# The first stage of a two-layer step: modulation loads in 1 KB runs, and five tiles of 128 tokens for the narrow projection

## The chip, the cores and the metric

The kernel runs on one core of a Trainium2 chip. The metric is the device time of one execution in microseconds (us). In the tables of the profile PE is the matrix engine (TensorE), DVE the vector engine, ACT the scalar engine, POOL the GpSimd engine and SP the engine that issues most of the DMAs.

## The reference

Two layers, the first a stick-breaking attention, the second a gated linear attention, work on 512 prompt tokens and 8 x 16 sample tokens, 640 tokens in all, with a model width of 2048, in float32. Each layer begins like this:

```
shift, scale, gate = jnp.split(c @ w_ada[i] + b_ada[i], 3, axis=-1)
h = rmsnorm(x, norm_g[i]) * (1 + scale[:, None]) + shift[:, None]
...
q, k, v, zg = jnp.split(h @ w_in, 4, axis=-1)
...
x = x + gate[:, None] * y
```

`c` has 9 rows (one for the prompt, 8 for the samples), and `w_ada[i]` is 2048 x 6144. Layer 0 has `w_in` of 2048 x 8192. Layer 1 has it 2048 x 6160, with its own `q`, `k`, `v`, `r` and a 16-wide decay input. The outputs are the normed activations, the new keys and values, and the states.

## The kernel before

Activations stand with the model width on the partitions: `xT` and `h` are 16 k-tiles of 128 rows by 640 tokens. Every float32 product is made of three matmuls on a split operand: `halves` makes `hi` by a cast on ACT and `lo = x - hi` on DVE, and a product is hi*hi, hi*lo and lo*hi, accumulated in PSUM.

**The first stage** loads x, transposes it, and makes the row scales (to about 30 us). It then makes shift and scale of layer 0 in pieces (`ada0`, `ada_mod`). A piece takes the columns of n k-tiles (n/2 lower ones, j, and the same upper ones, j + 8), for shift and scale each, over all 2048 rows of `w_ada`. A load into a ring tile `ar` is 128 partitions by 4 blocks of 64n columns, so that an uninterrupted run is 256n bytes: 512 bytes for n = 2, 1 KB for n = 4. Narrow matmuls (L178, 32 columns stationary, each quarter of PE's columns its own block) add them up in a PSUM bank; a DVE copy (`ada_r`, L181) and transposes by PE (L185) follow, then DVE, POOL and ACT make `mod`, the shifted and scaled k-tiles j and j + 8 (`scaled`, L247 to L253), and `part_up` splits them: the lower k-tile in two halves of 320 tokens, the upper whole. `part_up` also stores a half in DRAM (`h21_d`), on SP's queue. `add_up` makes sums and differences of quarters and their splits, which only later products read (`by_sevens`, which makes a product of 2 x 2 blocks from seven smaller ones).

Beside this runs `six` (L454): the first 512 columns of v, for which the 640 tokens stand as stationary tiles and the weights stream with 512 columns. For each j it needs the splits of k-tiles j and j + 8, and makes 6 token tiles x 2 k-tiles x 3 = 36 matmuls. The token tiles are 128, 128, 64, 128, 128 and 64 wide, since the lower k-tiles are held in halves of 320; the six accumulators hold five banks `mm` and the bank `z`. After the last j, L753 evacuates and SP stores (`v01`); then `by_sevens` (L520) takes the next projections.

The order on PE is the program's own: `drive` yields after each token tile, and `side.tick` puts in the next step of `ada0` when the planner's clock `pe["now"]` has passed its due time. `pace` sets such a time from the loads asked for so far, `side.every` the least distance of such steps, and `by` charges each matmul to that clock. `until` fills with side work until the planned `ready` time of j. SP, ACT, DVE and POOL take their instructions in an order that a scheduler makes.

**Layer 1** calls `six` again with all the k-tiles near at hand, the order of ACT, DVE and POOL being that of the code; its accumulators are evacuated as `vhi` and `vlo` (L1233), whose tiles have one buffer each, and stored before the next are made.

Of the kernel before, what the change touches and what calls it, by code (L numbers as in the profile page):

```python
# [15 lines left out]
P = 128  # L16
D = 2048
KT = D // P
NP = 512
# [22 lines left out]
def hybrid_step_kernel(ctx: ExitStack, tc: tile.TileContext, A: dict, O: list):  # L42
# [4 lines left out]
    dve = nc.vector  # L47


    pe = {"now": 0.0}  # L50

    mm, turn_block = nc.tensor.matmul, nc.tensor.transpose

    def by(l, r):

        n = r.free_size()
        if l.dtype == F32R:
            pe["now"] += n / 2400 + 0.0133
        elif l.free_size() <= 32:
            pe["now"] += n / 2400 + 0.01  # L60
        else:
            pe["now"] += n / 600 + 0.005
        return r
# [310 lines left out]
    class Quarters:  # L374
# [1 line left out]


        def __init__(self):
            self.lower, self.upper, self.whole = [None] * 8, [None] * 8, [None] * 8
            self.sums, self.exact = [[None] * 8 for _ in range(4)], [None] * 8  # L380

        def rows(self, kt, t0, w):
# [7 lines left out]

        def scale(self, i, j, xT, bc, pool=None):

            ts = self.exact[j] = [xT[kt] if pool is None else pool.tile([P, T], F32, tag="mod", name="mod", bufs=3)
                                  for kt in (j, 8 + j)]
            for t, kt in zip(ts, (j, 8 + j)):
                scaled(t, i, kt, xT[kt], bc)

        def part_up(self, i, j):

            (a0, a1), b = [self.exact[j][0][:, c] for c in hs], self.exact[j][1]  # L400
            store(h21_d[i][:, j, :], a1)
            self.lower[j], self.upper[j] = slot(j, (P, 2, HALF)), slot(8 + j, (P, 2, HALF))
            self.whole[j] = slot(16 + 2 * j), slot(17 + 2 * j)
            halves(self.lower[j][:, 0], self.lower[j][:, 1], a0)
            halves(self.upper[j][:, 0], self.upper[j][:, 1], a1)
            halves(*self.whole[j], b)

        def add_up(self, j, pool, places, gp=()):

# [19 lines left out]
                    self.upper[n + e] = slot(8 + n + e, (P, 2, HALF))  # L429
                    halves(self.upper[n + e][:, 0], self.upper[n + e][:, 1], r[:, e])  # L430

    tiles6 = [(0, P), (P, P), (256, 64), (320, P), (448, P), (576, 64)]

    def six(h, w, n0, acc, until, asked):


        src = w.rearrange("(kt p) n -> p kt n", p=P)

        def piece(j):
            asked()  # L440
            return wpiece(src[:, j:j + 9:8, n0:n0 + 512], 2, 512)

        nxt = piece(0)
        yield
        for j in range(8):
            until(j)
            wh, wl = nxt
            if j < 7:
                nxt = piece(j + 1)
            for i, (t0, n) in enumerate(tiles6):  # L450
                for e in range(2):
                    hi, lo = h.rows(j + 8 * e, t0, n)
                    for l, r, first, last in ((hi, wh, True, False), (hi, wl, False, False), (lo, wh, False, True)):
                        mm(acc[i][:n, :], l, by(l, r[:, e, :]), start=j == 0 and e == 0 and first,  # L454
                           stop=j == 7 and e == 1 and last)
                yield

# [216 lines left out]
    with tc.tile_pool(name="st", bufs=1, reuse_waits="tile") as st:  # L674
        for n, t in (("sh", sh_t), ("sc", sc_t)):
            t[0] = st.tile([P, KT, NSEQ], F32, name=f"{n}0")

        raw = {}
        crow = st.tile([120, P], F32, name="crow")
        c9 = st.tile([P, NSEQ, KT], F32, name="c9")  # L680
        for a in range(TOK):
            for hf in range(2):
                raw[a, hf] = sp.tile([P, 1024], F32, tag=f"s{2 * a + hf}", name="xr")
                load(raw[a, hf], x_src(a)[:, 1024 * hf:1024 * hf + 1024])
            if a == 0:
                load(crow[0:32, :], A["norm_g"].rearrange("l (k d) -> (l k) d", d=P))
                load(crow[32:48, :], A["gla_norm_g"].rearrange("l (k d) -> (l k) d", d=P))
                load(crow[48:56, :], A["gla_b_a"].rearrange("l (k d) -> (l k) d", d=P))
                load(crow[56:120, :], A["b_ada"][:, :2 * D].rearrange("l (k d) -> l k d", d=P))
                load(c9[:, 0, :], A["c_prompt"][0].rearrange("(p kt) -> p kt", kt=KT))  # L690
                load(c9[:, 1:, :], A["c_sample"].rearrange("r (p kt) -> p r kt", kt=KT))
        dve.tensor_copy(cT[:, :, :NSEQ], c9.rearrange("p r kt -> p kt r"))

        xT = [slot(kt if kt < 8 else 2 * kt, dt=F32, name="xT") for kt in range(KT)]
        bc = st.tile([P, T], F32, name="rstd_bc")
        for a in range(TOK):
            ss4 = st.tile([P, 4], F32, tag="ss4", name="ss4", bufs=2)
# [12 lines left out]
            rstd_row(st, ss, bc, a)  # L710
            if a == 2:
                tp = bank("tp")
                nc.tensor.transpose(tp[:, :120], crow, ident[:120, :120])
                dve.tensor_copy(cols, tp[:, :120])


        pe["now"] = 30.0
        come = {"n": 0}
        ready = {}

        def pace(n):
            come["n"] += n
            return max(0.0, 24.0 + 1.9 * come["n"] - pe["now"])

        def ring(tags):
            n = 0
            while True:
                tag = tags[n % len(tags)]
                yield ad_ring() if tag is None else sp.tile([P, 1024], F32, tag=tag, name="ar")
                n += 1  # L730

        early = ring(["s10", "s11", "s12", "s13", "s14", "s15", None, None])
        late = ring(["s12", "s13", "s14", "s15", None, None])
        last = ring(["s14", "s15", None, None])

        def ada0():
            for k0, n, r in ((0, 2, early), (1, 2, early), (2, 4, early), (4, 4, early), (6, 2, late), (7, 2, last)):
                yield from ada_mod(ad, lambda: next(r), 0, k0, n, "tp", 2, pace)
                for j in range(k0, k0 + n // 2):
                    h1.scale(0, j, xT, bc, st)  # L740
                    h1.part_up(0, j)
                    h1.add_up(j, st, (f"s{2 * j}", f"s{2 * j + 1}"))
                    ready[j] = pe["now"] + 6.5

        side.every = 1.0
        side.add(ada0())
        acc = [bank("mm") for _ in range(5)] + [bank("z")]
        drive(six(h1, w_in0, 2 * D, acc, lambda j: side.until(lambda: ready.get(j, 1e9) <= pe["now"]),
                  lambda: pace(1)))
        side.finish()  # L750
        for i, (t0, n) in enumerate(tiles6):
            t = slot(8 + i, (P, 512), F32, "v01")
            (dve.tensor_copy if i % 2 else nc.scalar.copy)(t[:n, :], acc[i][:n, :])  # L753
            for p in range(2):
                store(v_d[p][t0:t0 + n, :], t[:n, 256 * p:256 * p + 256])
            np_ = max(0, min(t0 + n, NP) - t0)
            if np_:
                store(vp_rows[t0:t0 + np_, 0:512], t[:np_, :])
            if np_ < n:
                store(vs_rows[max(t0, NP) - NP:t0 + n - NP, 0:512], t[np_:n, :])  # L760


    def rest_of_ada():
# [351 lines left out]
    with tc.tile_pool(name="o0", bufs=1, reuse_waits="tile") as po, ExitStack() as only_d:  # L1115
# [55 lines left out]
            if j == 6:  # L1171
                halves(wa[:, :, :16], wa[:, :, 16:], r)

        acc = [bank("mm") for _ in range(5)] + [bank("z")]
        gemm = six(h2, w_in1, 2 * NK, acc, until, lambda: None)
        next(gemm)
        side.finish()
# [14 lines left out]
        def make(j):  # L1192
            if j < 7:
                h2.scale(1, j + 1, xT, bc)
            if j < 8:
                h2.part_up(1, j)


        wa = pm.tile([P, 512], F32R, name="wa").rearrange("p (k n) -> p k n", k=KT)
# [23 lines left out]
        add_up()  # L1223
        queries = plain(h2, src, [(P * hh, leave_q(hh)) for hh in range(2)])

        for i, (t0, n) in enumerate(tiles6):
            if i == 2:
                next(queries)
            parts = [pm.tile([P, 512], F32R, tag=t, name=t) for t in ("vhi", "vlo")]
            halves(parts[0][:n, :], parts[1][:n, :], acc[i][:n, :])  # L1230
            for d in range(2):
                store(gv_d[0][d][t0:t0 + n, :], parts[d][:n, :].bitcast(F32))
        alr = pm.tile([96, 2, HALF], F32R, name="alr")  # L1233
        for nt in range(2):
            x = low[nt][:32, :HALF]
# [540 lines left out]
```

## Time and profile before

| | |
|---|---|
| time, median of 3 runs | 2637.93 us (2637.6 to 2638.26) |
| the profiled execution, its own time | 2633.23 us |
| its span (1.83 us lie around it) | 2631.4 us |
| PE busy | 2475.0 us, 94% of the span |
| DVE, ACT, POOL busy | 61%, 39%, 10% |
| DMA moved | 503.83 MB, mean 191 GB/s |

The span is divided by the profile in 40 slices of 66 us. PE is busy for nine tenths or more in nearly all of them; the slices in which it isn't are the first (6 tenths) and a few about the two attention stages. The views read here are the busy time in stretches, the instructions in order of time for one engine, the waits, and the chain of work that ended last.

### The profile page before, as it was taken

To read this page: it belongs to the slowest core of one execution; us is meant where nothing else is said; L and a number is where in the kernel's file an instruction comes from. 1 tells how busy PE (TensorE), PEld (TensorE's weight loads), DVE (VectorE), ACT (ScalarE), POOL (GpSimd) and SP (SyncE) were. 2 spreads that over 40 slices of the span, in tenths; PEclk is the share of its full clock that TensorE was granted. 3 is DMA by queue.
4 is the path that set the end of the run, shared out by engine and by line. 5 is a ranking of instruction groups with operands and counts; after the bars stand their busy time and mean duration, and the time that the engine had idled before them with its cause. 6 is when DMAs were issued, how large, how long until landed. Compare 5 with 4: busy or idle time off the path is not lost.

```text
span 2631.4 us, 43839 instructions
## 1 busy us (share of the span) xinstructions
PE 2475.0 (94%) x17393; PEld 2162.9 (82%) x17393; DVE 1597.8 (61%) x2429; ACT 1017.4 (39%) x1804; POOL 261.3 (10%) x537
## 2 busy tenths in 40 slices
PE   6999999999999989999999989999999998787998
PEld 4569999989999989787777767999999987675776
DVE  4555556555556646766776666666677564555556
ACT  4332222222223335555453453333333362464333
POOL 1200000000000000000000050000000134424300
PEclk8899999999999999999999989999999998999999
DMA  9966666766674366666665633344543577846554
GB/s 314 314 208 222 216 216 202 232 209 216 198 237 144 118 215 212 227 209 221 209 225 173 189 110 108 90 119 117 144 119 105 170 226 233 280 158 209 203 196 148
DMA packets 495358, 503.83 MB, mean 191 GB/s; under 512 B 26090, under 2 KB 416626, under 8 KB 495026
## 3 DMA queue, kind: packets, MB, share of 16 engines
q1 hardware_dynamic: 477426, 446.49, 53.7%
q0 software_dynamic: 17728, 54.54, 6.3%
q8 instruction: 137, 2.24, 0.3%
q14 instruction: 67, 0.55, 0.1%
HBM read 411.16 MB, written 89.78 MB: 190 GB/s over the span
## 4 chain that ended last, share of the span: by engine, by line
PE 74%; DMA 7%; DVE 7%; issue 5%; ACT 3%; POOL 3%; SPq 1%; ACTq 0%; POOLq 0%; DVEq 0%
PE ps_mm L520 41%; PE ps_mm L619 8%; PE ps_mm L454 4%; PE ps_mm L356 3%; PE ps_mm L575 3%; PE ps_tp L976 2%; PE ps_tp L944 1%; PE ps_z L920 1%; PE ps_z L178 1%; DMA ar<-in_w_ada_dram 1%; PE ps_z L218 1%; DVE wl L136 1%; PE ps_tp L1021 1%; PE ps_mm L1747 1%; PE ps_z L989 1%
## 5 line engine op out<-in xcount | busy, mean ns | idle before, releaser
L520 PE MATMUL ps_mm<-sums,wh 128*128 128x320 f32 x2880 | 642.2, 311 | 0.4 <-ACT wh L135 0.4
L520 PE MATMUL ps_mm<-h,wh 128*128 128x320 f32 x2160 | 484.7, 313 | 5.5 <-ACT wh L135 3.8
L520 PEld LDWEIGHTS ps_mm<-sums,wh 128*128 128x128 f32 x2880 | 479.4, 188 | 12.2 <-issue 9.0
L520 PE MATMUL ps_mm<-sums,wl 128*128 128x320 f32 x1440 | 445.3, 309 | 0.7 <-DVE wl L136 0.7
L520 PEld LDWEIGHTS ps_mm<-h,wh 128*128 128x128 f32 x2160 | 360.4, 188 | 22.0 <-issue 13.3
L136 DVE TENSOR_TENSOR wl<-wr,wh 128x1024 fp32r<-128x1024 f32 x191 | 233.9, 1226 | 234.0 <-ACT wh L135 233.0
L135 ACT CAST wh<-wb 128x1024 fp32r<-128x1024 f32 x180 | 188.9, 1049 | 460.2 <-PE ps_mm L520 389.6
L520 PE MATMUL ps_mm<-h,wl 128*128 128x320 f32 x1080 | 334.8, 310 | 2.2 <-DVE wl L136 2.2
L135 ACT CAST wh<-wr 128x1024 fp32r<-128x1024 f32 x191 | 200.1, 1049 | 330.4 <-PE ps_mm L520 201.1
L520 PEld LDWEIGHTS ps_mm<-sums,wl 128*128 128x128 f32 x1440 | 270.4, 188 | 1.0 <-DVE wl L136 1.0
L136 DVE TENSOR_TENSOR wl<-wb,wh 128x1024 fp32r<-128x1024 f32 x180 | 219.9, 1222 | 66.0 <-ACT wh L135 63.4
L619 PE MATMUL ps_mm<-wh,ogh 128*128 128x512 f32 x450 | 199.7, 444 | 15.5 <-ACT ogh L135 11.0
L575 PE MATMUL ps_mm<-h,wh 128*128 128x320 f32 x896 | 209.1, 321 | 3.5 <-DVE out L526 2.1
L520 PEld LDWEIGHTS ps_mm<-h,wl 128*128 128x128 f32 x1080 | 203.5, 188 | 2.9 <-DVE wl L136 2.9
L619 PE MATMUL ps_mm<-wh,ogl 128*128 128x512 f32 x450 | 180.4, 401 | 0.6 <-DVE ogl L136 0.4
L619 PE MATMUL ps_mm<-wl,ogh 128*128 128x512 f32 x450 | 180.4, 401 | 0.0
L575 PEld LDWEIGHTS ps_mm<-h,wh 128*128 128x128 f32 x896 | 153.0, 193 | 16.0 <-issue 11.3
L575 PE MATMUL ps_mm<-h,wl 128*128 128x320 f32 x448 | 140.9, 315 | 2.3 <-DVE wl L136 2.3
L454 PE MATMUL ps_mm<-wh,h 128*128 128x512 f32 (+1 forms) x320 | 113.4, 425 | 10.0 <-ACT h L135 7.1
L619 PEld LDWEIGHTS ps_mm<-wh,ogh 128*128 128x128 f32 x450 | 87.8, 195 | 41.7 <-ACT ogh L135 12.2
L858 DVE TENSOR_TENSOR_SCAN k<-k,zero_c 128x544 f32<-128x544 f32 (+4 forms) x96 | 93.3, 975 | 29.7 <-ACT k L854 17.5
L619 PEld LDWEIGHTS ps_mm<-wh,ogl 128*128 128x128 f32 x450 | 86.6, 192 | 21.7 <-DVE ogl L136 1.8
(306 smaller groups left out, 3912.4 us busy)
## 6 DMA issues: line engine op xcount, KB each, us to landing
ar<-in_w_ada_dram SPq DMA_DIRECT2D x160, 512.0 KB
wb<-in_sb_w_in_dram SPq DMA_DIRECT2D x84, 512.0 KB
kc<-in_cache_sb_k_dram SPq DMA_DIRECT2D x64, 512.0 KB
vc<-in_cache_sb_v_dram SPq DMA_DIRECT2D x64, 512.0 KB
wb<-in_gla_w_in_dram SPq DMA_DIRECT2D x51, 512.0 KB
wr<-in_gla_w_in_dram SPq DMA_DIRECT2D x45, 512.0 KB
wr<-in_sb_w_in_dram SPq DMA_DIRECT2D x44, 512.0 KB
ar<-in_w_ada_dram SPq DMA_DIRECT2D x64, 256.0 KB
```

Source lines behind the costliest of these rows:

```text
L135: nc.scalar.copy(hi, x)
L136: dve.tensor_tensor(lo, x, hi.bitcast(F32), op=ALU.subtract)
L178: mm(acc[32 * q:32 * q + 32, :w], cT[:, kt + m, :], by(cT[:, kt + m, :], rs[m // each][:, m % each, q, :]), start=kt + m == 0, stop=kt + m ...
L218: mm(acc[32 * j:32 * j + 32, :256], cT[:, kt + m, :], by(cT[:, kt + m, :], r[:, 256 * j:256 * j + 256]), start=kt + m == 0, stop=kt + m == ...
L356: mm(acc[a], l[:, c], by(l[:, c], r[:, k2, :]), start=kt == k0 and first, stop=kt == k0 + nk - 1 and last)
L454: mm(acc[i][:n, :], l, by(l, r[:, e, :]), start=j == 0 and e == 0 and first, stop=j == 7 and e == 1 and last)
L520: mm(acc, l[:, k, :], by(l[:, k, :], r), start=start and k == 0 and first, stop=k == 7 and last, skip_group_check=True)
L575: mm(acc[nt], l[:, k, :], by(l[:, k, :], r), start=k0 == 8 and k == 0 and first, stop=k0 == 0 and k == 7 and last)
L619: mm(acc, l, by(l, r[:, e, :]), start=i == 0 and e == 0 and first, stop=i == 1 and e == 1 and last)
L858: dve.tensor_tensor_scan(kr, kr, zeros[:, :w], 1.0, ALU.mult, ALU.add)
L920: mm(z[:, :n], q[:, hh, qs], by(q[:, hh, qs], k[:, hh, :n]), start=True, stop=True)
L976: turn_block(tp[:, P * c:P * c + P], block(kc[:, c, P * hh:P * hh + P]), ident)
```

## The change

1. The pieces of `ada0` are (first k-tile, n) = (0,4), (2,4), (4,4), (6,2), (7,2) in place of (0,2), (1,2), (2,4), (4,4), (6,2), (7,2). Pieces of n = 4 come in groups of four loads (2 MB) in place of two; the accumulators of the pieces alternate between the banks `z` and `tp`.
2. `six` takes five tiles of 128 tokens in the order 0, 1, 3, 4, 2: 30 matmuls for each j. The middle tile (tokens 256 to 383) lies across the two halves of a lower k-tile, so `part_up` makes a further split of these 128 tokens, `middle` (a cast on ACT, a subtraction on DVE). Layer 1 does the same, and there `middle` stands in the buffers `vhi` and `vlo` by turns.
3. `part_up`'s store of `h21` goes to ACT's queue in place of SP's.
4. `add_up` is put off by planned time (`side.after`), the planner charges other costs (`pace` 18 + 1.4 n for 24 + 1.9 n, `side.every` 0.5 for 1.0, half the cost for L178), and `mod` has 4 buffers for 3.
5. The evacuations are five with three stores each in place of six with nineteen stores in all.

```diff
-            return max(0.0, 24.0 + 1.9 * come["n"] - pe["now"])
+            return max(0.0, 18.0 + 1.4 * come["n"] - pe["now"])
...
-        def part_up(self, i, j):
+        def part_up(self, i, j, two):
...
-            store(h21_d[i][:, j, :], a1)
+            nc.scalar.dma_start(out=h21_d[i][:, j, :], in_=a1)
...
+            self.middle[j] = two[:, :P], two[:, P:]
+            halves(*self.middle[j], self.exact[j][0][:, 256:384])
...
-            for i, (t0, n) in enumerate(tiles6):
+            for a in (0, 1, 3, 4, 2):
                 for e in range(2):
-                    hi, lo = h.rows(j + 8 * e, t0, n)
+                    hi, lo = h.middle[j] if (a, e) == (2, 0) else h.rows(j + 8 * e, P * a, P)
...
-            for k0, n, r in ((0, 2, early), (1, 2, early), (2, 4, early), (4, 4, early), (6, 2, late), (7, 2, last)):
-                yield from ada_mod(ad, lambda: next(r), 0, k0, n, "tp", 2, pace)
-                for j in range(k0, k0 + n // 2):
+            for i, (k0, n, r) in enumerate(((0, 4, early), (2, 4, early), (4, 4, early), (6, 2, late), (7, 2, last))):
+                yield from ada_mod(ad, lambda: next(r), 0, k0, n, ("z", "tp")[i % 2], 4 if n == 4 else 2, pace)
+                js = range(k0, k0 + n // 2)
+                for j in js:
                     h1.scale(0, j, xT, bc, st)
-                    h1.part_up(0, j)
-                    h1.add_up(j, st, (f"s{2 * j}", f"s{2 * j + 1}"))
-                    ready[j] = pe["now"] + 6.5
+                    h1.part_up(0, j, st.tile([P, 256], F32R, tag="middle", name="middle", bufs=2))
+                    ready[j] = pe["now"] + 6.5 + 3.0 * (j - k0)
+                    side.after(2.0 + 2.5 * (j - k0), lambda j=j: h1.add_up(j, st, (f"s{2 * j}", f"s{2 * j + 1}")))
...
-        side.every = 1.0
+        side.every = 0.5
...
-        acc = [bank("mm") for _ in range(5)] + [bank("z")]
+        acc = [bank("mm") for _ in range(5)]
...
-                h2.part_up(1, j)
+                h2.part_up(1, j, pm.tile([P, 512], F32R, tag=("vhi", "vlo")[j % 2], name="middle")[:, :256])
```

On PE, ahead of the first product of `six`, the order before has a piece of n = 2 (64 narrow matmuls), its transpose and half of the next piece (32):

```order
L178 MATMUL ps_tp<-ar,cT 32x128 x64
L185 MATMUL ps_tp<-ident,ada_r 128x128
L178 MATMUL ps_tp<-ar,cT 32x128 x32
L454 MATMUL ps_mm<-wh,h 128x512
L454 MATMUL ps_mm<-wl,h 128x512
```

After the change a piece of n = 4, its two transposes and a quarter of the next piece stand there:

```order
L178 MATMUL ps_z<-ar,cT 32x256 x64
L185 MATMUL ps_tp<-ident,ada_r 128x128 x2
L178 MATMUL ps_tp<-ar,cT 32x256 x16
L454 MATMUL ps_mm<-wh,h 128x512
L454 MATMUL ps_mm<-wl,h 128x512
```

So the first product stands behind 16 loads of 512 KB and four more, where it stood behind 8 and four.

On SP at the end of the first stage, the order before has the first three weights of `by_sevens` (`wb`) behind the stores of the first evacuated tile:

```order
L74 DMA vd_148<-v_1779 128x256
L74 DMA vd_149<-v_1779 128x256
L74 DMA out_dram<-v_1779 128x512
L71 DMA wb<-in_sb_w_in_dram 128x8x128 x3
L74 DMA vd_148<-v_1784 128x256
```

After the change they stand behind the stores of all five tiles, of which these are the last:

```order
L74 DMA vd_148<-v_1684 128x256
L74 DMA vd_149<-v_1684 128x256
L74 DMA vd_148<-v_1674 128x256
L74 DMA vd_149<-v_1674 128x256
L74 DMA out_dram<-v_1674 128x512
L74 DMA out_dram<-v_1684 128x512
L71 DMA wb<-in_sb_w_in_dram 128x8x128 x4
```

`v_1674` is the tile of the middle tokens, whose product is the last of `six`; four stores stand between its evacuation and the weights' loads.

On ACT, for a j of the first stage, the order before has activations (`mod`) and the casts of the splits alone:

```order
L253 ACTIVATE mod<-mod,sh_166 128x512 x2
L135 CAST h<-mod 128x320 x2
L135 CAST h<-mod 128x640
L135 CAST sums<-sx 128x320 x4
L135 CAST wh<-wr 128x1024
```

After the change the store of `h21` (`h_0_156`) stands among them, ahead of a cast that `six` needs, and so does the cast of `middle`; the casts of `sums` stand behind the second j's:

```order
L253 ACTIVATE mod<-mod,sh_166 128x512 x2
L135 CAST h<-mod 128x320
L135 CAST middle<-mod 128x128
L401 DMA h_0_156<-mod 128x320
L135 CAST h<-mod 128x320
L253 ACTIVATE mod<-mod,sh_166 128x512 x2
```

Behind the first stage the order on every engine is what it was, but for layer 1's `six` and its evacuation.

## Rows read from the trace of the kernel before

**Rows 1.** The page: busy us, share of the span and instructions of PE.
```profile
PE 2475.0 (94%) x17393; PEld 2162.9 (82%) x17393; DVE 1597.8 (61%) x2429; ACT 1017.4 (39%) x1804; POOL 261.3 (10%) x537
```

**Rows 2.** Busy us per stretch of 10 us, each engine; at the end PEclk, DMA share, GB/s.
```profile
0.00:10.00 10.00, 3.91 (x18) 3.58 (x18) 3.26 (x16) 4.65 (x12) 1.74 (x9) 1.00 0.72 209
10.00:20.00 10.00, 7.18 (x35) 6.39 (x34) 5.07 (x25) 8.63 (x31) 1.10 (x2) 0.59 1.02 375
...
30.00:40.00 10.00, 6.35 (x155) 4.14 (x155) 3.67 (x10) 1.31 (x2) 2.06 (x5) 0.95 1.03 311
...
90.00:100.00 10.00, 10.00 (x54) 6.60 (x57) 9.62 (x21) 5.14 (x12) 4.17 (x4) 0.82 1.09 384
...
150.00:160.00 10.00, 6.41 (x53) 3.92 (x51) 3.90 (x13) 3.03 (x6) 2.83 (x5) 0.93 0.36 124
```

**Rows 3.** PE in order of time: start, us, line, tiles, [idle before <- releaser].
```profile
47.23 0.80 PE L454 MATMUL ps_mm<-wh,h 128*128 128x512 f32 x1
...
54.76 0.62 PE L454 MATMUL ps_mm<-wh,h 128*128 128x512 f32 x2
...
55.44 0.62 PE L454 MATMUL ps_mm<-wh,h 128*128 128x512 f32 x2
...
59.08 1.07 PE L178 MATMUL ps_tp<-ar,cT 128*32 128x256 f32 x16
...
83.70 0.44 PE L185 MATMUL ps_tp<-ident,ada_r 128*128 128x128 f32 x2 [0.55 <-DVE ada_r L181]
...
158.82 0.80 PE L454 MATMUL ps_mm<-wh,h 128*128 128x512 f32 x1 [3.59 <-ACT h L135]
...
170.90 0.57 PE L520 MATMUL ps_mm<-h,wh 128*128 128x320 f32 x2 [0.16 <-ACT wh L135]
```

**Rows 4.** All engines in order of time, behind the transposes at 83.70 us.
```profile
88.65 0.76 POOL L252 TENSOR_TENSOR mod<-mod,sh 128x128 f32<-128x128 f32 x2
...
90.88 0.81 DVE L136 TENSOR_TENSOR h<-mod,h 128x640 fp32r<-128x640 f32 x1
...
91.95 1.22 SPq L74 DMA_DIRECT2D h<-mod  x1
```

**Rows 5.** SP's waits in the first 181 us: us in total, times, longest.
```profile
SPq L71 <- PE ps_tp L178: 38.2, 24, 5.8
```

**Rows 6.** The chain of waits at the end of the first stage: start, us, what.
```profile
163.93 0.45 SPq L74
...
164.47 0.41 SPq L71
...
165.75 6.97 DMA wb<-in_sb_w_in_dram
...
172.81 1.23 DVE t L488
...
179.42 5.69 PE ps_mm L520 x37
```

**Rows 7.** Layer 1, busy us in two stretches; columns as in rows 2.
```profile
1540.00:1550.00 10.00, 8.05 (x23) 5.84 (x24) 7.66 (x10) 6.62 (x12) 9.22 (x15) 0.61 0.34 117
1550.00:1600.00 50.00, 50.00 (x221) 37.37 (x220) 30.33 (x43) 23.33 (x39) 20.35 (x30) 1.00 0.34 101
```

**Rows 8.** The chain of waits through the end of layer 1's `six` and its evacuation.
```profile
1600.95 1.38 PE ps_z L454 x6
1602.34 6.82 PE ps_mm L454 x30
...
1610.32 0.58 ACT vhi L135
...
1614.61 2.06 DMA gv<-vhi
...
1621.71 0.48 DVE alr L1238
...
1656.95 8.12 PE ps_mm L520 x43
```

More of the change, by code (lines that the diff above doesn't have):

```diff
@@ L47, in hybrid_step_kernel @@
     dve = nc.vector
-    pe = {"now": 0.0}
+    pe = {"now": 0.0, "quad": 4800}
     mm, turn_block = nc.tensor.matmul, nc.tensor.transpose
@@ L59, in by @@
         elif l.free_size() <= 32:
-            pe["now"] += n / 2400 + 0.01
+            pe["now"] += n / pe["quad"] + 0.01
         else:
@@ L378, in __init__ @@
         def __init__(self):
-            self.lower, self.upper, self.whole = [None] * 8, [None] * 8, [None] * 8
+            self.lower, self.upper, self.whole, self.middle = [None] * 8, [None] * 8, [None] * 8, [None] * 8
             self.sums, self.exact = [[None] * 8 for _ in range(4)], [None] * 8
@@ L391, in scale @@
         def scale(self, i, j, xT, bc, pool=None):
-            ts = self.exact[j] = [xT[kt] if pool is None else pool.tile([P, T], F32, tag="mod", name="mod", bufs=3)
+            ts = self.exact[j] = [xT[kt] if pool is None else pool.tile([P, T], F32, tag="mod", name="mod", bufs=4)
                                   for kt in (j, 8 + j)]
@@ L430, in again @@
                     halves(self.upper[n + e][:, 0], self.upper[n + e][:, 1], r[:, e])
-    tiles6 = [(0, P), (P, P), (256, 64), (320, P), (448, P), (576, 64)]
     def six(h, w, n0, acc, until, asked):
@@ L449, in six @@
                 nxt = piece(j + 1)
-            for i, (t0, n) in enumerate(tiles6):
+            for a in (0, 1, 3, 4, 2):
                 for e in range(2):
-                    hi, lo = h.rows(j + 8 * e, t0, n)
+                    hi, lo = h.middle[j] if (a, e) == (2, 0) else h.rows(j + 8 * e, P * a, P)
                     for l, r, first, last in ((hi, wh, True, False), (hi, wl, False, False), (lo, wh, False, True)):
-                        mm(acc[i][:n, :], l, by(l, r[:, e, :]), start=j == 0 and e == 0 and first,
+                        mm(acc[a], l, by(l, r[:, e, :]), start=j == 0 and e == 0 and first,
                            stop=j == 7 and e == 1 and last)
@@ L750, in hybrid_step_kernel @@
         side.finish()
-        for i, (t0, n) in enumerate(tiles6):
-            t = slot(8 + i, (P, 512), F32, "v01")
-            (dve.tensor_copy if i % 2 else nc.scalar.copy)(t[:n, :], acc[i][:n, :])
-            for p in range(2):
[L755 to L760, printed above, removed]
+        pe["quad"] = 2400
+        v01 = []
+        for i in range(5):
+            v01.append(slot(8 + i, (P, 512), F32, "v01"))
+            (dve.tensor_copy if i % 2 else nc.scalar.copy)(v01[i], acc[i])
+            for p in range(2):
+                store(v_d[p][P * i:P * i + P, :], v01[i][:, 256 * p:256 * p + 256])
+            store(vp_rows[P * i:P * i + P, 0:512] if i < 4 else vs_rows[:, 0:512], v01[i])
     def rest_of_ada():
@@ L1172, in until @@
                 halves(wa[:, :, :16], wa[:, :, 16:], r)
-        acc = [bank("mm") for _ in range(5)] + [bank("z")]
+        acc = [bank("mm") for _ in range(5)]
         gemm = six(h2, w_in1, 2 * NK, acc, until, lambda: None)
@@ L1224, in hybrid_step_kernel @@
         queries = plain(h2, src, [(P * hh, leave_q(hh)) for hh in range(2)])
-        for i, (t0, n) in enumerate(tiles6):
+        for i in range(5):
             if i == 2:
@@ L1229, in hybrid_step_kernel @@
             parts = [pm.tile([P, 512], F32R, tag=t, name=t) for t in ("vhi", "vlo")]
-            halves(parts[0][:n, :], parts[1][:n, :], acc[i][:n, :])
+            halves(parts[0], parts[1], acc[i])
             for d in range(2):
-                store(gv_d[0][d][t0:t0 + n, :], parts[d][:n, :].bitcast(F32))
+                store(gv_d[0][d][P * i:P * i + P, :], parts[d].bitcast(F32))
         alr = pm.tile([96, 2, HALF], F32R, name="alr")
```

## Prediction

> **What bounds the kernel now.** I read the page first, then PE's stretches, then PE in order of time with the waits, then the chain. PE is busy for 94% of the span [rows 1], so a change pays in two ways only: fewer PE columns where PE is full, or fewer waits where it isn't. The change touches one place of each sort.
>
> The first stage is the one where PE waits. Up to about 110 us the DMA queues are full: a share of 1.03 at 311 GB/s while pieces in runs of 512 bytes come, 1.09 at 384 GB/s while those of 1 KB come [rows 2]. Behind that the share falls, to 0.36 and 124 GB/s at 150 to 160 us [rows 2], and PE still isn't full (6.41 of 10). There the loads wait for ring tiles (SP waited 38.2 us for PE's narrow matmuls [rows 5]) and `six` waits for its splits, 3.59 us before j = 7 [rows 3]. So the second half is bound by latency: loads, narrow matmuls, transposes, splits, products, one piece after the other. `six` runs from 47.23 to 170.74 us (170.90 less the 0.16 idle before it) [rows 3], steady work of `by_sevens` begins at 179.42 [rows 6].
>
> Layer 1's `six` is the other sort: 50.00 of 50 us busy at a full clock [rows 7], 6.82 + 1.38 = 8.20 us for each j [rows 8].
>
> **The change part by part.**
>
> *Fewer matmuls.* A tile of 64 tokens streams the same 512 columns as one of 128: six of them 1.38 us, thirty of any width 6.82 [rows 8], 0.23 each. The first stage shows the same price at a full clock, 0.68 us between one triple's start and the next [rows 3]. Five tiles for six take 6 x 8 = 48 matmuls out of each layer's `six`: 48 x 0.228 = **10.9 us** of PE work in each.
>
> *Layer 1.* PE is full there, so the 10.9 us come out of the path at first. Nothing else is near taking over: POOL is full only at the start (9.22 of 10, then 20.35 of 50 [rows 7]), which is 29.6 us in the two stretches for some seven j, 4.2 each, below the new 6.85; ACT's 23.33 and DVE's 30.33 of 50 grow by a cast and a subtraction of 128 columns for each j, whose price lies between nothing and the 0.5 us of a split of 320. What is given back: the evacuation. Its rounds are a cast `vhi` (0.58), `vlo` and a store (2.06) that frees the buffers [rows 8]. Before, the third of six began as `six` ended (1610.32), and `alr` came at 1621.71: four rounds in 11.4 us, 2.8 us each. Now the first `vlo` waits for the last group of products, since the last `middle` stands in its buffer; it comes 0.3 us ahead of the end, four more rounds of 2.8 and 1.4 to `alr` follow: 12.3 us for some 11.2, about 1.1 us lost. The store on ACT's queue stands ahead of the first casts once: 0.35. I take **-9.5 us**, between -10.5 (nothing lost) and -6 (a further round and a half). What follows the evacuation is a chain of DVE work to 1656.95 [rows 8], which moves with it.
>
> *First stage, first pair.* The first product now waits for a pair of 4. By 20 us 5.84 MB had come (2.09 + 3.75 [rows 2]). The loads of x, the first piece and three weights make 15.4 MB; the other 9.6 MB at 0.38 MB per us [rows 2] land at 45.2 us. The last narrow matmuls (1.07 for two loads [rows 3]) and the copy bring the transposes to 46.8. The splits of a pair lag behind: from 83.70 POOL's last part ended at 89.4 and the last `lo` stood at 91.7 [rows 3, 4], 8 us. Four more loads stand ahead of the first product (to 52.1). `six` so begins at 52 to 56, against 47.23: 5 to 8 us later, but with two j in hand.
>
> *First stage, the rest.* I walked the changed order with these durations: 6.85 us of products for each j, 1.07 for each half group of narrow matmuls, 8 us from a transpose to the last split, 0.38 MB per us for pieces of 4, 0.30 for pieces of 2. j = 0 ends at 63.9 and j = 1 at 71.9; the second pair's transposes come at 75, j = 2 waits to 84.3 and j = 3 ends at 100.8; the third pair is turned at 104, its j = 4 held by loads of the next piece to 110; j = 6 ends at 137.8, j = 7 waits for its split to about 141, and `six` ends at **148** against 170.74. The bounds are 142 (none of the waits for loads between the tiles) and 156 (each of the last three pieces late by 2 to 3 us). So -23 there, of which 10.9 are the matmuls, the rest fewer chains of piece, transposes and splits in series: five for six, the early ones of two j each.
>
> *The end of the stage gives back.* Before, three weights were asked for at 164.47, 6.3 us before `six` ended, behind one tile's stores; the last of them landed at 172.72 and steady work began at 179.42, 8.7 us behind the end of `six` [rows 3, 6]. Now all stores stand ahead. Four of them follow the last evacuation: 0.85 + 4 x 0.45 [rows 6] = 2.6 us behind the end of `six`. The third weight lands 8.25 us after the first is asked for (164.47 to 172.72), so at +10.9, and 172.81 to 179.42 [rows 6], less the copy of 0.6 that stood between, is 6.0 more: +16.9, perhaps +16.3 with lighter queues. That is 7.6 us worse. The bounds: +5 (loads land in half the time on emptier queues) and +10. Net of the first stage: -23 + 7.6 = **-15**, between -21 and -5.
>
> *Edits costed at nothing.* `add_up` put off: its sums are needed by `by_sevens` only, and DVE is near full only just behind a pair's transposes (9.62 of 10 at 90 to 100 us, 3.90 at 150 to 160 [rows 2]). The store on ACT: 0.4 us of issue, covered by ACT's idle time, more if it has to wait (below).
>
> *Rule against trace.* Runs of 1 KB came at 384 GB/s where runs of 512 bytes came at 311, at a full share both times [rows 2]. The Trainium skill, DMA: Bandwidth & Descriptors, Specifications, has it that 512 bytes is already enough for line rate, so that longer runs would bring nothing; by that rule the first pair would land at 51.4 for 45.2, and the sum would be about -11. The trace disagrees.
>
> *Sum.* -15 - 9.5 = -24.5 against the profiled execution: 2633.23 - 24.5 = 2608.7. That execution was 4.7 below the median of the runs, so the forecast for a median is 2637.93 - 24.5 = **2613**. Between the two places the order is unchanged and PE full, so a shift carries through.
>
> **The rivals.**
>
> *A: the longer runs load no faster.* The 384 came in a stretch of mixed transfers, which speaks for it; a share above 1 at both rates speaks against it. At 0.305 MB per us a pair needs 8.39 MB + 2 weights, 31 us, a piece of 2 15.5: the first pair at 51.4, then 82, 113, 129, 144.5, `six` ends at 162, steady at 178. First stage -1.5, total -11: 2627.
>
> *B: the latency of pairs and the wait for the weights eat the first stage's gain.* For it: j = 2, 4 and 6 each wait 8 us or more behind their transposes, and a pair of splits shares POOL and DVE; the clock may also fall in longer waits (0.59 was granted at 10 to 20 us, PE busy for 7.18 of 10 [rows 2]). Against it: the loads come in the meantime. First stage 0, layer 1 -9.5: 2628.
>
> *C, slower: the store on ACT's queue holds its casts.* In the built order the store carries a wait for an earlier `ada` load of the same semaphore in most of the j of the first stage, and ACT takes no cast until then. A queued load was in flight for 6.97 us [rows 6]. By my walk these loads have landed by then, within 1 us. If instead each of the eight stores held ACT for 4 us, 32 us would stand on the path, and the total would be +7.5: 2645. It decides from 3 us for each store. On SP the same store took 1.22 us [rows 4], with no cast behind it.
>
> *D: the five tiles don't shorten layer 1*, because the split of `middle` or POOL sets the pace at 8.2 us for each j: -15 alone, 2623. Against it the busy shares in rows 7.
>
> **How the numbers follow.** Forecast 0.62 (2605 to 2621), A 0.11, B 0.14, D 0.06, C 0.07. Two kernels can be told apart from about 0.2%, 5.3 us. Forecast, A, B and D all lie below 2632.6 in their middles, but the upper ends of A and B reach past it: faster 0.86, same 0.08, slower 0.06. The range goes from 2602 (first stage -21, layer 1 -10.5, 4 more for unknowns) to 2631, which takes in A, B and D and leaves out C.
>
> **What the profile would show.** Right: the first product at 52 to 56 us, no idle of PE over 9 us behind it, the end of `six` at 142 to 156, the first `wb` asked for 2 to 3 us behind it, and `by_sevens` steady by 159 to 172; in layer 1 6.85 us for each j, and `alr` about 1612. Wrong: below 350 GB/s from 30 to 70 us (A); PE waiting over 10 us for `h` at j = 2 or 4 with full queues or not (B); ACT waiting at L401 for DMA by several us, with `h` behind it (C); over 7.5 us for each j in layer 1 (D). An end of `six` as forecast with a time that isn't shorter would say that PE is not what carries the shift on.

## The result, and the profile after

The changed kernel takes **2618.85 us** (median of 4 runs, 2617.74 to 2618.94) against 2637.76 of the kernel before: a ratio of 0.9932, 95% interval 0.9915 to 0.9949, or 18.9 us less by the medians. The forecast was 2613, 24.5 less, in a range of 2602 to 2631. A later timing in five rounds gave 0.9941 (0.9921 to 0.9961). So it is faster, as forecast, by some 16 to 19 us, and the sum was too large by 6 to 9. It was also put together wrongly: of its two terms layer 1 came out as forecast, the first stage nearly vanished, and some 5 us came from stages where none were expected.

The profiled execution took 2618.87 us, with a span of 2617.2 us. PE's busy time is 26.6 us less than in [rows 1]:

```profile
PE 2448.4 (94%) x17169; PEld 2144.5 (82%) x17169; DVE 1601.5 (61%) x2436; ACT 1021.0 (39%) x1819; POOL 259.5 (10%) x537
```

The first stage in stretches of 10 us; columns as in [rows 2], the last three being the granted clock, the DMA share and GB/s:

```profile
30.00:40.00 10.00, 5.23 (x56) 1.07 (x48) 1.32 (x2) 1.05 (x1) 0.00 (x0) 0.81 1.08 384
40.00:50.00 10.00, 6.44 (x50) 1.43 (x50) 2.19 (x9) 0.43 (x1) 1.11 (x2) 0.50 1.08 388
50.00:60.00 10.00, 8.16 (x34) 3.66 (x35) 8.84 (x16) 6.87 (x16) 6.36 (x11) 0.50 1.09 384
...
70.00:80.00 10.00, 9.39 (x88) 6.19 (x85) 2.30 (x3) 1.05 (x1) 0.00 (x0) 1.00 0.80 270
...
160.00:170.00 10.00, 1.84 (x5) 1.44 (x6) 1.60 (x2) 1.05 (x1) 0.00 (x0) 0.63 0.98 302
```

Two things are to be seen. The loads now come at 384 to 388 GB/s where pieces of 512 byte runs came at 311 [rows 2], as forecast. And the clock is at 0.50 (1.2 GHz of 2.4) from 40 to 60 us, behind a stretch in which PE was busy for 5.23 of 10 us, so that `six` begins at half clock. At 160 to 170 us PE is nearly idle: that is the end of the stage.

PE in order of time, in the first stage; columns as in [rows 3]:

```profile
47.51 0.69 PE L185 MATMUL ps_tp<-ident,ada_r 128*128 128x128 f32 x2 [0.55 <-DVE ada_r L181]
...
53.63 0.79 PE L454 MATMUL ps_mm<-wh,h 128*128 128x512 f32 x1
...
55.78 0.80 PE L454 MATMUL ps_mm<-wh,h 128*128 128x512 f32 x1 [0.50 <-ACT h L135]
...
59.23 1.05 PE L454 MATMUL ps_mm<-wh,h 128*128 128x512 f32 x2
60.08 0.63 PE L454 MATMUL ps_mm<-wl,h 128*128 128x512 f32 x1
60.51 0.63 PE L454 MATMUL ps_mm<-wh,h 128*128 128x512 f32 x1
61.06 3.15 PE L178 MATMUL ps_tp<-ar,cT 128*32 128x256 f32 x32
...
72.32 0.62 PE L454 MATMUL ps_mm<-wh,h 128*128 128x512 f32 x2
72.78 0.39 PE L454 MATMUL ps_mm<-wl,h 128*128 128x512 f32 x1
73.01 0.62 PE L454 MATMUL ps_mm<-wh,h 128*128 128x512 f32 x2
...
80.26 0.44 PE L185 MATMUL ps_tp<-ident,ada_r 128*128 128x128 f32 x2 [0.87 <-DVE ada_r L181]
...
90.28 1.22 PE L454 MATMUL ps_mm<-wh,h 128*128 128x512 f32 x2 [0.79 <-DVE h L136]
...
111.86 0.44 PE L185 MATMUL ps_tp<-ident,ada_r 128*128 128x128 f32 x2 [0.87 <-DVE ada_r L181]
...
120.27 0.79 PE L454 MATMUL ps_mm<-wh,h 128*128 128x512 f32 x1
...
150.43 0.73 PE L454 MATMUL ps_mm<-wh,h 128*128 128x512 f32 x2 [0.28 <-DVE h L136]
...
175.25 0.46 PE L520 MATMUL ps_mm<-sums,wh 128*128 128x320 f32 x2
```

The first transposes stand at 47.5 (forecast 46.8), the first product at 53.6 (52 to 56). At 59.23 a triple takes 1.28 us to the next (59.23 to 60.51), at 72.32 it takes 0.69: half clock (granted 0.50) and full (1.00). The second pair's transposes then come at 80.3 where the forecast had 75; the rows from 90.28 on are read further below.

The chain of waits at the end of the stage:

```profile
152.16 6.01 PE ps_mm L454 x25
158.20 0.60 ACT v L756
...
161.18 0.46 SPq L74
...
161.74 0.40 SPq L71
...
162.96 6.65 DMA wb<-in_sb_w_in_dram
169.63 1.24 DVE t L488
...
173.40 1.06 ACT wh L135
174.49 1.24 DVE wl L136
175.76 7.01 PE ps_mm L520 x46
```

`six` ends at 158.2 (forecast 148, before 170.7). The first weight is asked for 3.6 us behind that (161.74), behind the last stores, and the steady work of `by_sevens` begins at 175.76, 17.6 us behind the end of `six`, where it was 8.7 before [rows 6]. So 12.5 us are gained and 8.9 given back.

Layer 1, a stretch in which PE is full, and the chain through the end of its `six`, as [rows 7, 8]:

```profile
1550.00:1600.00 50.00, 50.00 (x232) 40.75 (x231) 33.76 (x49) 26.27 (x48) 17.17 (x25) 1.00 0.39 120
```

```profile
1559.92 35.34 PE ps_mm L454 x155
...
1595.36 0.70 DVE vlo L136
1596.08 2.07 DMA gv<-vlo
...
1608.46 0.69 DVE vlo L136
1609.18 0.88 DVE alr L1237 x2
```

155 products take 35.34 us, 0.228 each and 6.84 for each j. The first `vlo` stands at 1595.36, 0.6 us ahead of the end of `six`, and `alr` 13.3 us behind it, where the forecast had 12.3.

### The profile page after: what moved, and what is told of

Its sections match the earlier page's. It is cut to its first block, busy times and chain, and to the rows that moved or that the text cites. A ratio compares the mean times of both kernels' runs of the same rounds, so it can differ in the third digit from the quotient of the medians.

```text
span 2617.2 us, 43380 instructions
## 1 busy us (share of the span) xinstructions
PE 2448.4 (94%) x17169; PEld 2144.5 (82%) x17169; DVE 1601.5 (61%) x2436; ACT 1021.0 (39%) x1819; POOL 259.5 (10%) x537
## 4 chain that ended last, share of the span: by engine, by line
PE 73%; DMA 9%; DVE 7%; issue 4%; ACT 3%; POOL 2%; SPq 1%; ACTq 0%; POOLq 0%; DVEq 0%
PE ps_mm L520 40%; PE ps_mm L619 8%; PE ps_mm L454 4%; PE ps_mm L356 3%; PE ps_mm L575 3%; PE ps_tp L975 2%; PE ps_z L178 1%; DMA ar<-in_w_ada_dram 1%; DVE wl L136 1%; PE ps_tp L943 1%; PE ps_z L919 1%; PE ps_z L218 1%; PE ps_tp L1020 1%; PE ps_mm L1746 1%; PE ps_tp L1344 1%
## 5 line engine op out<-in xcount | busy, mean ns | idle before, releaser
L619 PE MATMUL ps_mm<-wh,ogh 128*128 128x512 f32 x450 | 199.1, 442 | 15.0 <-ACT ogh L135 11.7
L575 PEld LDWEIGHTS ps_mm<-h,wh 128*128 128x128 f32 x896 | 150.8, 190 | 15.6 <-issue 10.9
L454 PE MATMUL ps_mm<-wh,h 128*128 128x512 f32 x288 | 102.0, 420 | 11.1 <-ACT h L135 8.0
```

The source lines that it names most:

```text
L454: mm(acc[a], l, by(l, r[:, e, :]), start=j == 0 and e == 0 and first, stop=j == 7 and e == 1 and last)
L575: mm(acc[nt], l[:, k, :], by(l[:, k, :], r), start=k0 == 8 and k == 0 and first, stop=k0 == 0 and k == 7 and last)
L619: mm(acc, l, by(l, r[:, e, :]), start=i == 0 and e == 0 and first, stop=i == 1 and e == 1 and last)
```

## Where the time went, stage by stage

By the first and last products of each stage in PE's order of time, two profiles of the kernel before and three of the changed one (us). Behind the last mixer another 127.5 us follow in every profile:

```
                                        before          changed                 mean
start to by_sevens' first sums          178.2  178.0    175.3  177.9  175.3     -1.9
by_sevens, to its last product          781.3  782.2    780.4  778.9  779.4     -2.2
attention and w_out, to layer 1's six   582.5  586.9    583.1  580.9  581.6     -2.8
layer 1's six, to by_sevens' first sums 119.9  119.4    109.7  110.1  110.2     -9.7
by_sevens, to the last mixer            471.7  470.0    470.2  470.3  471.4     -0.2
the last mixer, first to last product   370.4  373.9    371.0  370.2  374.2     -0.4
```

Rows of PE that the first and fourth lines rest on, from the kernel before and then from the changed one (its first sums stand above, at 175.25):

```profile
178.16 0.56 PE L520 MATMUL ps_mm<-sums,wh 128*128 128x320 f32 x2 [0.45 <-ACT wh L135]
...
1541.95 0.79 PE L454 MATMUL ps_mm<-wh,h 128*128 128x512 f32 x1 [3.54 <-ACT h L135]
...
1661.83 0.46 PE L520 MATMUL ps_mm<-sums,wh 128*128 128x320 f32 x2
```

```profile
1538.69 0.79 PE L454 MATMUL ps_mm<-wh,h 128*128 128x512 f32 x1 [3.54 <-ACT h L135]
...
1648.39 0.45 PE L520 MATMUL ps_mm<-sums,wh 128*128 128x320 f32 x2
```

The sum is -17.2, which the timings bear out. Layer 1 is 9.7 of it (forecast 9.5), the first stage 1.9 (forecast 15). The 2.8 of the attention lies within what two profiles of the same kernel differ by (4.4 there), the 2.2 of `by_sevens` a little outside (0.9 between the two profiles before, 1.5 among the three after); of that part no run tells the cause.

## The experiments

**The changed kernel again, and the kernel before again.** No edit; two timings of the changed kernel, with a profile each, and a second profile of the kernel before. From here on the end of `six` is the start of its last product, some 0.2 us before its end.

> The changed kernel itself, on one chip with the kernel before. In the two profiled executions the changed kernel is 14.4 us shorter (2633.23 to 2618.87), by the medians 18.9. Theory: the profiles are right, and the medians differ because the kernel before was mostly measured on another chip: 13 to 15 us shorter here, ratio 0.9945 to 0.995. Rival: the medians are right, and the profiled execution of before was a fast one: 18 to 19 us, ratio 0.993.

> The changed kernel itself, timed in five rounds against the kernel before. The two profiled executions lie 14.4 us apart, the medians of the first two jobs 17.4 and 18.9. Theory (the stages account for about 14 to 15, and the rest is spread): 13 to 18 us shorter, ratio 0.993 to 0.995.

> The kernel before, for a second profile of it: how far its stages move from one execution to the next. Theory (stage times that agree in the profiles are worth about 1 to 2 us): six ends at 169 to 172 us, sums of by_sevens at 177 to 180, layer 1's six lasts 68.5, and the last stage (from its first products to its last) varies by a few us, 366 to 375. Rival (its first stage moves by 5 us or more, so that the differences read off single profiles mean little).

The ratios were 0.9935 (0.9914 to 0.9956) and 0.9941 (0.9921 to 0.9961), 17.4 and 16.9 us by the medians. The second profile of the kernel before has the end of `six` at 169.8 and the first sums at 178.0 (170.6 and 178.2 in the first), layer 1's `six` within 1.2 us, the attention 4.4 and the last mixer 3.5 us longer. So a stage time of the first stage is good to 1 to 3 us, and the difference between the two shown profiles, 14.4, was low by chance in the attention and the mixer.

**The stores of the evacuation on POOL's queue.** The term of the sum that "gives back".

```diff
-                store(v_d[p][P * i:P * i + P, :], v01[i][:, 256 * p:256 * p + 256])
-            store(vp_rows[P * i:P * i + P, 0:512] if i < 4 else vs_rows[:, 0:512], v01[i])
+                move(v_d[p][P * i:P * i + P, :], v01[i][:, 256 * p:256 * p + 256])
+            move(vp_rows[P * i:P * i + P, 0:512] if i < 4 else vs_rows[:, 0:512], v01[i])
```

> The changed kernel, but the fifteen stores of the first stage's evacuation go to POOL's queue, so that on SP nothing stands ahead of by_sevens' first weights but other loads. Theory (the end of the stage gives back 8.9 us because the weights are asked for behind the stores): the weights are asked for about 5 us ahead of the end of six, steady work of by_sevens begins 8 to 10 us behind that end in place of 17.6, and the kernel is 7 to 9 us shorter than the changed one. Rival (the weights wait for buffers or for full queues anyway): 0 to 2 us.

2609.87 us, ratio to before 0.9911 (0.9884 to 0.9938), 7.3 less than the changed kernel on the same chip. The chain of waits has no store and no DMA left between the end of `six` and the weights' casts:

```profile
153.35 6.03 PE ps_mm L454 x25
...
159.88 1.06 ACT wh L135
160.94 0.02 issue
160.96 1.24 DVE wl L136
...
166.14 5.99 PE ps_mm L520 x37
```

The first sums come at 168.3, 9.1 us behind the end of `six` for 17.3 in the changed kernel: 8.2 us, nearly all of the 8.9 to 9.7 given back. The theory holds.

**Five tiles alone, and in layer 1 alone.** The kernel before with the five tiles and the split of the middle one, and nothing else; then the same for layer 1 only.

```diff
+    tiles5 = [(0, P), (P, P), (384, P), (512, P), (256, P)]
...
-            for i, (t0, n) in enumerate(tiles6):
+            for i, (t0, n) in enumerate(tiles):
                 for e in range(2):
-                    hi, lo = h.rows(j + 8 * e, t0, n)
+                    hi, lo = h.middle[j] if (t0, n, e) == (256, P, 0) else h.rows(j + 8 * e, t0, n)
```

> The kernel before with five tiles in both layers and nothing else of the change: pieces, groups, pace and the store of h21 as before. Read by the first stage alone (end of six, first product of sums), since the scheduler also orders a few instructions of the last stage in another way here. Theory (before, six waits for the pieces, so 1.37 us less for each j is only partly seen; the pieces of two j bring the rest): six ends at 164 to 167 us for 170.7 before and 158 to 161 in the changed kernel; by_sevens steady 17 us behind it, as in the changed kernel, since here too the weights stand behind all stores. Rival (the 10.9 us of matmuls are all of the first stage's gain): six ends at about 160.

> The kernel before with five tiles of 128 tokens in layer 1 alone, the first stage as it was. Theory (layer 1 gives 10.9 us less about 1 us at its evacuation, on its own): 9 to 10.5 us shorter than before, 6.85 us for each j. Rival (part of what shows at the end of layer 1 comes from the first stage, or the split of the middle tile sets the pace): 0 to 5 us.

The kernel with five tiles in both layers was timed once, at 2623.97 us, and is read by its stages. Its first stage's `six` ends at 165.4: by this one profile 5.2 of the 12 us are the tiles, the rest the pieces and their order. And the first sums come at 181.6, 3.4 us later than before, since here too SP has the weights behind all stores:

```profile
167.80 0.46 SPq L74
168.25 0.05 issue
168.35 0.41 SPq L71
...
169.58 6.70 DMA wb<-in_sb_w_in_dram
```

So it is the fewer tiles, not the pieces, that moved the weights behind the stores: the scheduler put them there once the evacuation had five tiles. In the first stage the five tiles alone were no gain, and by this profile a loss of some 3 us, about what two profiles of one kernel can differ by.

With five tiles in layer 1 alone the kernel took 2630.29, ratio 0.9982 (0.9968 to 0.9996): 4.2 less, not 9 to 10.5. Layer 1's `six` gains what it should: 57.6 us (68.4 before, 57.1 in the changed kernel). But from its start to the first sums it is 112.3 us (119.9 before, 109.7 in the changed kernel), so some 2 us of the miss stand right behind `six`, and no run tells why. The first product of the last mixer comes at 2123.3 for 2133.5, 10.2 earlier, of which 2.5 were there before layer 1's `six` began. The last mixer then takes 377.1 us for 370.4 and 373.9. In this kernel, and not in the changed one, the scheduler ordered about a dozen instructions of that stage in another way on ACT, DVE and POOL (loads of the state further up, an activation later). The next run below has the same order there and took 376.0; ten profiles with the old order took 363.9 to 374.2. But five tiles in both has nearly all of the new order too and took 371.4, and the run with the store of `h21` on SP's queue has the rest of it (a load of the state further up on POOL) and took 371.6. So the order is a weak suspect: it wasn't tried by itself, and chance may do as much.

**The first pair in two pieces.** `(0, 2), (1, 2)` in place of `(0, 4)` in the changed kernel; timed once, 2625.79 us.

> The changed kernel with the first pair in two pieces of n = 2 (512 byte runs) as before. Read by the first stage alone. Theory (the pair starts later, but with two j in hand): the first product at about 47 us for 54 to 56, the load rate at 30 to 40 us back to about 310 GB/s for 384, the transposes of the second pair 3 to 6 us later than the changed kernel's 80 to 82, and six ends 1 to 5 us later than the changed kernel's 158 to 161. Rival (the first pair costs what it delays): six ends 4 us or more earlier.

The loads came slower, as in [rows 2]; the two stretches, for 384 and 388 above:

```profile
30.00:40.00 10.00, 5.77 (x125) 2.87 (x116) 3.12 (x10) 1.35 (x2) 2.03 (x5) 0.85 1.03 305
40.00:50.00 10.00, 5.74 (x76) 1.71 (x72) 1.98 (x5) 2.24 (x6) 1.15 (x2) 0.50 1.00 302
```

That is the place of rival A. Runs of 512 bytes cost a fifth of the rate here, with the queues full both times (a share of 1.00 to 1.03, and 1.08). By the Trainium skill (DMA: Bandwidth & Descriptors, Specifications) transfers of 512 bytes are enough for line rate; neither this trace (302 to 305 GB/s) nor that of the kernel before (311) agrees.

The rest of this run is inconclusive. The first product came at 54.1, not at 47, because with the planner's new costs PE's order has the whole second piece ahead of it, and the end of `six` at 159.2 lies within the changed kernel's 157.0 to 160.6. Here ACT stood still for a load at the store of `h21`:

```profile
48.48 0.38 ACTq L401 DMA_DIRECT2D h<-mod  x1
48.90 0.82 ACT L135 CAST h<-mod 128x320 fp32r<-128x320 f32 x2 [7.67 <-DMA ar<-in_w_ada_dram]
```

**The store of `h21`.** On SP's queue again, first in the changed kernel, then in the fastest one below.

```diff
-            nc.scalar.dma_start(out=h21_d[i][:, j, :], in_=a1)
+            store(h21_d[i][:, j, :], a1)
```

> The changed kernel with the store of h21 on SP's queue, as before. Theory (the store on ACT costs its issue and under 1 us of waits in all): six ends within 1.5 us of the changed kernel's 158 to 161, layer 1's six within 0.5 of its 57.1 us. Rival (the store holds ACT, and with it the splits): six ends 3 us or more earlier here. It could also be later here, if the store's wait then stands ahead of loads on SP.

> The run with the evacuation's stores on POOL's queue and the sample part of the modulation on DVE, but with the store of h21 on SP's queue again. There ACT waited 5.6 us at two of these stores for a load that uses the same semaphore, with casts behind them. Theory (the store on ACT holds the splits where its semaphore's load is late): these waits go, the third pair's first products (j = 4) come 2 to 4 us earlier behind its transposes, six ends 2 to 4 us earlier than 157.4. Rival (other waits, loads and POOL-free splits, end last there): under 1 us, or a loss if the store now stands ahead of loads on SP.

In the changed kernel (timed once, 2622.3 us) it makes no difference: `six` ends at 158.8 (157.0 to 160.6 with ACT's store) and lasts 57.1 in layer 1. In the second pair of runs two waits of 2.4 and 3.3 us at that store went away, and `six` ended at 156.7 for 157.4, with the transposes of the last piece at 144.7 for 145.3: under 1 us, by the rival; 2601.76 against 2602.59 by the medians. So the wait of rival C exists, up to 7.67 us long, but where it was seen and taken away `six` ended less than 1 us earlier.

**The clock.** The changed kernel with three, then two (the cut below), extra matmuls of 512 columns behind the narrow ones of each of the first 20 loads. Their sums go to a bank that `six` starts anew. The run with two was timed once.

```diff
+                if i == 0 and (k0 == 0 or (k0 == 2 and kt == 0)):
+                    for _ in range(2):
+                        mm(warm["acc"], warm["x"][:, :P], warm["x"], start=True, stop=True, skip_group_check=True)
```

> The changed kernel with three extra matmuls of 512 columns (their result is overwritten) behind the narrow matmuls of each of the first 20 loads, where PE waits for the next load, so that PE's clock has less reason to fall ahead of six's first products. Theory (my walk of the first stage was 10 us short because it priced every product at the full clock, and 8.5 us of the changed kernel's six are surplus at half clock): the granted clock at 40 to 60 us rises from 0.50 towards 1, the surplus of j = 0 (2.4 us) and about 1 us of slow narrow matmuls go, and the end of six and the kernel's end come 3 to 4 us earlier. Rival (the surplus lies beside waits for splits and loads): under 1 us. If the extra matmuls delay the narrow ones, the end comes later.

> As the run with three extra matmuls behind the narrow ones of each of the first 20 loads, but with two: with three PE had 1.33 us of work for each load, about what a load takes, and the first transposes came late (50.4). Read from the first transposes on. Theory (half clock makes six's first products and narrow matmuls slow on the path): the clock is 1.00 from 40 to 60 us, the first transposes come at 47.5 to 50 and the end of six 107 to 108.5 us behind them, for 108.9 to 111.4 in four profiles of the changed stage. Rival (the surplus is hidden by waits): 109 to 111.5.

With three, PE had no room left (9.84 of 10 us busy at 30 to 40), and the first transposes were late, at 50.4; it took 2620.73 us, no gain. With two, PE was as full there (9.95), and at 40 to 50 it was busy for 7.02 of 10 us; it took 2618.85 us. Its stretches are these, for a clock of 0.50, 0.50 and 0.82 in the changed kernel:

```profile
40.00:50.00 10.00, 7.02 (x60) 1.62 (x60) 0.42 (x1) 0.00 (x0) 0.00 (x0) 1.00 1.08 386
50.00:60.00 10.00, 7.92 (x48) 2.28 (x47) 8.32 (x19) 6.29 (x14) 6.82 (x11) 0.83 1.08 374
60.00:70.00 10.00, 9.93 (x75) 6.98 (x79) 7.55 (x18) 3.78 (x8) 0.64 (x1) 1.00 1.06 366
```

The end of `six` came 107.0 us behind the first transposes (107.3 with three), for 108.9 to 111.4 in five profiles with the changed kernel's `six`. That is as the theory had it. What was tried by this is the slow start alone: the first products of j = 2 and j = 4 stood at half clock in these runs too. The whole kernel isn't shorter, since the first transposes came at 50.1 and 50.4 here, for 47.5 to 50.3; whether by the extra work or by the loads, these two runs don't tell.

What a product at half clock costs can be summed. From the start of `six` to its end, with 0.228 us for each product at the full clock, what lies above it, the narrow matmuls and the rest (us). The ends of matmuls are modelled in the profile, so that some 2 us can go to "half clock" or to "idle"; the sum of the two is firm:

```
                        length   products   half clock   narrow   transposes   idle
before                  123.5    65.5       11.4         29.2     1.4          15.9
changed                 104.5    54.6        9.0         24.8     1.0          15.1
changed, second profile 105.5    54.6        9.0         24.6     1.0          16.2
changed, third          103.1    54.6        7.8         24.3     1.0          15.4
two extra matmuls       100.2    54.6        6.4         24.0     1.0          14.1
```

**The sample part of the modulation on DVE**, with the evacuation's stores on POOL's queue.

```diff
-                scaled(t, i, kt, xT[kt], bc)
+                scaled(t, i, kt, xT[kt], bc, dve if i == 0 else None)
```

> The changed kernel with the evacuation's stores on POOL's queue (as in the run before on that) and the first stage's sample part of the modulation on DVE in place of POOL. Theory (behind a pair's transposes six waits 8 to 10 us for splits, and POOL's serial part, 4.6 us for a pair, is the longest in that chain): the first product of j = 2 that needs the last split comes 2 to 3 us earlier behind the transposes, six ends 4 to 8 us earlier than with POOL, and the kernel is as much shorter than 2609.9. Rival (DVE is then the longer chain, being near full behind a pair): no gain or a loss of up to 3 us.

2602.59 us, ratio 0.9893 (0.9864 to 0.9922): the fastest kernel along with the same one with the store of `h21` on SP's queue (0.9881, 0.9852 to 0.9910). But not for the reason stated. The last split that j = 2 waits for came 9.2 us behind the transposes (79.06 to 88.24) for 10.0 (80.26 to 90.28), 0.8 earlier and not 2 to 3: DVE is now the serial part, 10.00 of 10 us busy at 80 to 90:

```profile
80.00:90.00 10.00, 5.10 (x37) 2.78 (x28) 10.00 (x29) 7.12 (x15) 0.00 (x0) 0.83 1.06 367
```

`six` ends at 157.4, 1.8 earlier than with POOL, but within the 157.0 to 160.6 of the changed kernel; the first sums come 3.2 earlier. The other 4 us of the medians come in the stages behind and are open; the last mixer took 363.9 in this profile, the least of all, with nothing changed there.

## Why the forecast was right in sign and too large

**Layer 1: right.** 10.9 us of PE work, less about 1 at the evacuation: 9.5 forecast, 9.7 measured (10.2 between the two profiles shown). PE stays full, ACT, DVE and POOL stay below it (the stretch of 1550 to 1600 us), and rival D is out.

**Loads: right.** 384 to 388 GB/s; first transposes 47.5 to 49.2 for 46.8. Rival A is out.

**The walk of `six`: the step that failed.** Forecast: 52 to 148, some 96 us. Measured: 103.1 to 105.5. The start was 1.5 to 3 us later than 52, within its bounds. The idle time of PE, 15 to 16 us, is what it was before (15.9), so rival B's longer waits are not the cause. What the walk lacked is above all the column "half clock": 7.8 to 9.0 us. I had priced every product of the new walk at 0.228, the price of a row at the full clock, and taken the old end, 170.74, from the trace, which holds 11.4 us of half clock. So a walk at full clock was set against a trace with both. The rows were at hand: in the profile before the clock was 0.82 and 0.93 in two of the stretches of [rows 2] in which `six` ran, and I named the clock in rival B as something that might come, when it was there already. Had I carried 10 us of it over, `six` would have ended at about 158.

Not all of that column is path, though. In the shown profile some 2 of its 9.0 us stand in j = 0 and j = 2 ahead of a wait for a split, where a faster product would only have waited longer; the other 6 to 7 stand behind such waits. Set beside the walk, piece by piece, the shown profile is slower by 3.7 us from the first product to the second pair's transposes (53.6 to 80.3, walk 52 to 75), where its first products stand at a clock of 0.50, by 0.7 from these to the last split of j = 2 (10.0 us for 9.3), by 1.9 to the third pair's transposes, by 2.4 from these to j = 4, which waits for loads (111.9 to 120.3, 8.4 us for 6), and by 1.6 over j = 4 to 6, where 3.2 us of half clock stand. It is faster by 1.7 over j = 7, whose splits came nearly in time (a wait of 0.28 in the row of 150.43; the walk had 3.2). So the wait for loads ahead of j = 4 is a second term that was put too small, and most of it was made good at j = 7, where the walk had a wait that didn't come.

Taken the other way, as a difference: products 10.9, narrow matmuls 4 to 5 (a piece of four stands ahead of the first product in place of a piece of two), half clock 2 to 4, idle nothing; the later start of `six` takes 6.4 to 8 back. That is the 12 us.

**The end of the stage: right in kind, a little short.** Forecast 7.6 us given back, measured 8.9 in the shown profile and 9.7 by the mean to the first sums; the weights were asked for 3.6 us behind the end, not 2.6. This term was read off the built order, and the run with POOL's queue shows nearly the whole of it.

By its own signs this part of the forecast failed: the end of `six` was to come at 142 to 156 us and came at 158.2, steady work by 159 to 172 and came at 175.8. So the first stage's -23 + 7.6 became -11.7 + 9.7 = -2, outside the -21 to -5 that was given for it. That is, within 2 us, the number that rival B had for the first stage (nothing gained), by way of the slow clock and the wait for the weights, both of which it names, and not by longer waits for splits. Layer 1 and the first stage alone make 11.6 us, which is 2626: inside the range, since that was wide, but with rivals A and B and not with the forecast's 2605 to 2621. That the total came out in there is owed to 5 us from stages that the forecast had at nothing and no run explains. It is luck.

**The store on ACT: right.** 0.33 us of issue each, one wait of 0.7 us. Rival C's price, 4 us at each of eight stores, was never met here, though single waits of 2.4 to 7.7 us in other orders show that its mechanism is real.

## What to carry to other kernels

Walk a changed order twice, once for the order before, and compare the two walks; a walk at ideal prices set against a measured end books every slow clock and small wait as gain. Where an edit removes tiles, look at what the scheduler then does with the transfers at the stage's end: a load that slips behind stores cost nearly as much here as the matmuls saved, and moving the stores to an idle engine's queue gave it back. A small edit can reorder a stage far away, so compare the orders there, and read stage times and not the total alone, when a variant of a scheduled kernel is judged.

## What the runs showed that was not expected

- Stages far from the change move by 3 to 5 us between two profiles of one kernel (attention 582.5 and 586.9, last mixer 370.4 and 373.9), which is as much as 0.2% of the kernel.
- Extra matmuls between the loads raised the granted clock from 0.50 to 1.00 at 40 to 50 us while PE's busy time only went from 6.44 to 7.02 of 10 us.
- An instruction that starts a DMA on ACT can wait for a load that another engine asked for: 7.67 us in one case, with casts queued behind it.
